# One core, a hybrid decoder layer: the keys' norms and scaling moved into the last projection of a head, the masks of the inverse issued one level ahead, the retention's decayed keys bound to program order

## Chip, core and metric

The kernel runs on one core of one Trainium2 chip. The metric is the device time of one execution in microseconds (us). Three runs of the kernel before gave 2976.19, 2977.47 and 2981.94 us, a median of 2977.47 us.

## What is computed

One step of a one-layer decoder on 2048 prompt rows, 16 learned meta rows in front of them, and 8 x 4 rows of sampling, 1024 wide. The residual stream goes through one combined input projection into two groups of four heads: retention, and gated DeltaNet. Then come an output projection, a layer norm, a SwiGLU feed-forward part of width 2816 and a last layer norm. The change lies in the DeltaNet group, with one line in the retention group. Cut to that:

```python
def l2_norm(x):
    return x * lax.rsqrt(jnp.sum(jnp.square(x), -1, keepdims=True) + RMS_EPS)
...
gk = l2_norm(conv[..., W:2 * W].reshape(bsz, L, H_GDN, HEAD_DIM))
beta = jax.nn.sigmoid(gb.astype(f32))
...
decay = jnp.exp(jnp.where(incl, G[..., :, None] - G[..., None, :], -jnp.inf))
kk = jnp.einsum('bnhid,bnhjd->bnhij', k, k)
lower = jnp.where(strict, kk * decay, 0.0) * beta[..., :, None]
a_mat = jnp.eye(C, dtype=q.dtype) + lower
...
sol = lax.linalg.triangular_solve(a_mat, rhs, left_side=True, lower=True, unit_diagonal=True)
...
k_d = k * jnp.exp(log_gamma[:, None] * (C - 1.0 - idx))[..., None]
```

The last line is of the retention group. A chunk is 128 rows.

## The kernel before

**Stages.** The attention part runs from the start to about 1310 us of the trace, the output projection and the feed-forward part fill the rest. The change touches the attention part only. It goes over four blocks (b0 to b3) of 512 prompt rows; b0 carries the 48 meta and sampling rows as well. In each block the projections of eight heads follow each other, in b0 to b2 as r0 g0 r1 g1 r2 g2 r3 g3 (r: retention, g: DeltaNet), in b3 as r0 g0 g1 r1 g2 g3 r2 r3.

**Projections fill PE.** A projection is a row of k-steps of three matmuls (L406), a product of high and low parts. A retention projection (`ret_proj`) takes tiles of 128 rows and eight k-steps of 256 columns each; a DeltaNet projection (`gdn_proj`) has four parts, q, k, v and the gate z, each of eight k-steps of 512 columns. After q, k and v come a convolution over four rows and a SiLU, on ACT and DVE (L860 to L871). `flip` (L804) transposes q or k on PE (L810), takes sums of squares on ACT (L813) and, for k, copies the transposed keys `kp` to SBUF on DVE (L817). It is called at step 5 of the k part for q, and at step 5 of the z part for k. Behind all four parts stand the norms: `rsqrt` (three Newton steps of small DVE instructions, L266 to L278) and the two scale vectors `gsk` (L875, L876).

**Chains lie among the projections.** When the projection of g is through, its chain (`gdn_chain`, `gdn_group`) starts. It is a generator that yields a nominal time from the list `LAT` after each piece; `advance` hands it the time of the k-steps that go by. So its pieces lie among the k-steps of the next projections, stretched by a factor from `pace`: 0.9 x 25 us x (heads until the next g) / `INVERSE`, for two heads 0.9 x 25 x 2 / 21 = 2.14. A chain begins with the decays (`mg` on DVE L918, L921 on PE, the exponential on ACT L925, two maskings on POOL L926 and L927), scales the keys (`kp`, DVE L935), transposes and scales v (PE L938, DVE L939), transposes the scaled keys (PE L943, ACT L945), forms kT x kT (PE L949) and the masked matrix `LT` (DVE L951). From it come `Z` and `U` on DVE (L960, L961), and on POOL, in one loop (L963), the six masked matrices `Lm` of the six levels. Each level then takes a product (L973), a correction on DVE (L975) and two products (L980, L982). Two refinements follow (L993 to L1003). In the second half of the chain the four chunks are scanned: L1035 and L1036 on PE, `r` on DVE (L1038), L1043 on PE, `u` on ACT, L1052 and L1054 on PE, the new state and `O` on DVE (L1053, L1055), `kt` on DVE (L1022). The second half of one head's chain runs beside the first half of the next one's.

**Other work on DVE and POOL there.** In b0 to b2 the layer norm of the next block's rows is issued during r1, g1, r2 and g2 at steps 18 and 26 (`LN_AT`), that is in the z part of g1 and of g2: statistics and multiplication on DVE (L289, L307), two additions on POOL (L309). A tile of a retention projection needs two rotary products on DVE (L571, L572) and an addition on POOL (L573). The retention chain (`ret_chain`) has in its `flip` the decayed keys `rkd` (DVE L634).

**What sets the order.** The code is traced in the order above, and then a scheduler lays each engine's instructions into a fixed row by its own estimate of when each can start: what was traced first goes first if it is ready, otherwise something later passes it. On the chip each engine takes its row strictly in order. `keep_in_program_order` binds an instruction behind the one that was traced last on its engine. PSUM tiles `w` have three buffers, the projections' `pj` two.

Of the kernel before, what the change touches and what calls it, by code (L numbers as in the profile page):

```python
# [8 lines left out]
F32 = mybir.dt.float32  # L9
# [4 lines left out]
ALU = mybir.AluOpType  # L14
# [4 lines left out]
HD = 128  # L19
# [220 lines left out]
class Builder:  # L240
# [372 lines left out]
    def ret_chain(self, b, h, qkvg, mixd):  # L613
# [12 lines left out]
        def flip(t):  # L626
            rows, c0, ch = tiles[t]
            pp = self.prt.tile([128, 4, 128], F32, tag="rt", name="rt")
            for a in range(2):
                nc.tensor.transpose(pp[:, a, :rows], qk[t][:, a, :], self.ident[:rows, :rows])  # L630
            qkT = mp.tile([128, 2, 128], F32, tag="rqkT", name="rqkT")[:, :, :rows]
            nc.scalar.copy(out=qkT, in_=pp[:, 0:2, :rows])
            kd = mp.tile([128, 128], F32, tag="rkd", name="rkd")[:rows]
            nc.vector.tensor_scalar(out=kd, in0=qk[t][:, 1, :], scalar1=col("kdm" if ch < 0 else "kd", rows), scalar2=None, op0=ALU.mult)  # L634
            st[t] = [pp, qkT[:, 0], qkT[:, 1], kd]
# [152 lines left out]
    def gdn_proj(self, b, h, G, out):  # L788
# [15 lines left out]
        def flip(a):  # L804

            for ts in sets:
# [7 lines left out]
                if a:  # L814
# [3 lines left out]
                    kps.append(kp)  # L818

        for piece in range(2):  # L820
            wh, wl = self.next_piece()
            for part in range(2):
# [9 lines left out]
                for (c0, n) in groups:  # L832
# [17 lines left out]
                if which < 3:  # L850
# [21 lines left out]
                    cv.append(o)  # L872
        rn = self.rsqrt(sq.rearrange("p a b -> p (a b)"), 2 * nt, 128, self.sm, 1.0, 4.0 * RMS_EPS).rearrange("p (a b) -> p a b", a=2)
        sk = self.sm.tile([128, 2, nt], F32, tag="gsk", name="gsk")
        nc.vector.tensor_scalar(out=sk[:, 0], in0=rn[:, 0], scalar1=HD ** -0.5, scalar2=None, op0=ALU.mult)  # L875
        nc.vector.tensor_tensor(out=sk[:, 1], in0=rn[:, 1], in1=G["sb"][:, :, h], op=ALU.mult)  # L876
        out += [cv, zg, sk, kps]

# [19 lines left out]
    def gdn_group(self, b, h, cv, zg, sk, kp, G, mixd, ts, tiles):  # L898
# [16 lines left out]


        mg = big("mg")[:R, :, :R]
        nc.vector.tensor_tensor(out=mg, in0=bc(M1), in1=G["g"][:R, ts[0]:ts[0] + m, h].unsqueeze(2).broadcast_to([R, m, R]), op=ALU.mult)  # L918
        pe = wide()
        for i in range(m):  # L920
            nc.tensor.matmul(pe[:R, i, :R], lhsT=U1, rhs=mg[:, i, :], start=True, stop=True)  # L921
        yield LAT[6]
        E = big("E", 2)[:R, :, :R]
# [3 lines left out]
        nc.gpsimd.tensor_tensor(out=E, in0=E, in1=bc(M1), op=ALU.mult)  # L927


        kp = kp[:R]  # L930
        vb = big("vb", 2, n=128)[:R]
        lane = lambda a: a.unsqueeze(2).broadcast_to([R, m, 128])
        here = slice(ts[0], ts[0] + m)
        cq = sk[:R, 0, here]
        nc.vector.tensor_tensor(out=kp, in0=kp, in1=lane(sk[:R, 1, here]), op=ALU.mult)  # L935
        p = wide()[:R, :m, :]
        for i in range(m):
            nc.tensor.transpose(p[:, i, :], v[:, col(i):col(i) + R], self.ident)  # L938
        nc.vector.tensor_tensor(out=vb, in0=p, in1=lane(G["sv"][:R, here, h]), op=ALU.mult)  # L939
        yield LAT[7]  # L940
        pk = wide()
        for i in range(m):
            nc.tensor.transpose(pk[:, i, :R], kp[:, i, :], idn)  # L943
        kT = big("kT", 2)[:, :, :R]
        nc.scalar.copy(out=kT, in_=pk[:, 0:m, :R])  # L945
        yield LAT[8]
        pl = wide()
# [13 lines left out]
        nc.vector.scalar_tensor_tensor(out=U, in0=L0, scalar=-1.0, in1=Ib, op0=ALU.mult, op1=ALU.add)  # L961
        for x in range(1, nl):
            nc.gpsimd.tensor_tensor(out=Lm[:, x - 1], in0=LT, in1=lvl(x), op=ALU.mult)  # L963
        yield LAT[9]
        pt = wide()[:R, :m, :R]
# [3 lines left out]
        for x in range(1, nl):  # L969
            yield LAT[10]  # L970
            py = wide()[:R, :m, :R]
            for i in range(m):
                nc.tensor.matmul(py[:, i, :], lhsT=Lm[:, x - 1, i, :], rhs=T[:, i, :], start=True, stop=True)  # L973
            Z = big("Z", 2, F16)[:R, :, :R]
            nc.vector.scalar_tensor_tensor(out=Z, in0=py, scalar=-1.0, in1=Ib, op0=ALU.mult, op1=ALU.add)  # L975
            yield LAT[11]
            pt = wide()[:R, :m, :R]
            pu = wide()[:R, :m, :R]
            for i in range(m):
                nc.tensor.matmul(pt[:, i, :], lhsT=U[:, i, :], rhs=Z[:, i, :], start=True, stop=True)  # L980
# [8 lines left out]
        nc.scalar.copy(out=V, in_=U)
        yield LAT[12]  # L990
        pe = wide()[:R, :m, :R]
# [5 lines left out]
        for it in range(2):  # L997
            yield LAT[13]
            pu = wide()[:R, :m, :R]
            for i in range(m):  # L1000
                nc.tensor.matmul(pu[:, i, :], lhsT=Er[:, i, :], rhs=V[:, i, :], start=True, stop=True)
            V = big(f"V{it}", 1, F32 if it else F32R)[:R, :, :R]
            nc.vector.tensor_tensor(out=V, in0=U, in1=pu, op=ALU.add)  # L1003
# [14 lines left out]
        for i in range(m):  # L1018
# [19 lines left out]
            nc.vector.scalar_tensor_tensor(out=r[:orow], in0=pp[:orow, 0, :], scalar=gc("ng", i, orow), in1=vb[:orow, i, :], op0=ALU.mult, op1=ALU.add)  # L1038
# [631 lines left out]
```

## Time and profile before

| what | value |
|---|---|
| median of three runs | 2977.47 us |
| the profiled execution | 2978.62 us |
| its span in the trace | 2976.8 us |
| mean granted clock of PE | 0.985 |

The profiled execution lies 0.04% above the median. Its span is 1.8 us shorter than its time. In the rows of the trace a time is counted from the start of the span; a DVE instruction's start can lie a few hundredths of a us before the end of the one ahead of it. A row of the timeline gives start, length, engine, line, operation, what it writes and reads, and in brackets the idle time ahead of it with what ended it.

### The profile page before, as it was taken

How to read it: one execution, taken by the hardware profiler on the slowest of the kernel's cores; microseconds unless marked ns; L12 is line 12 of the kernel's file. 1: busy time of each engine (PE TensorE's matmuls, PEld its weight loads, DVE VectorE, ACT ScalarE, POOL GpSimd, SP SyncE). 2: the span in 40 equal slices, each digit the busy share in tenths (PEclk: the TensorE clock that was granted, in tenths of full speed). 3: DMA queues.
4: the chain of work that ended last, by engine and by line, in shares of the span. 5: the costliest groups of instructions: out<-in, count | busy, mean ns of one | idle time of the engine just before them, and what ended most of it. 6: DMA issues, size and time to landing. Idle time of an engine off the chain costs nothing. (4 is left out here: it accounts for less than half of the span.)

```text
span 2976.8 us, 47482 instructions
## 1 busy us (share of the span) xinstructions
PE 2854.8 (96%) x17942; PEld 2550.5 (86%) x17942; DVE 1938.3 (65%) x4218; ACT 996.7 (33%) x2351; POOL 778.0 (26%) x757
## 2 busy tenths in 40 slices
PE   6999999999999999989989999999999999999997
PEld 6977888888888878877778999999999999989886
DVE  7777777776776676757776776667544444854447
ACT  2434344444444454432233333333211111321221
POOL 1312222221222112215544434433200101411111
PEclk8989999999999999999999999999999999999999
DMA  7544534444344333346768766667755555787762
GB/s 259 202 163 150 201 136 156 149 169 150 135 155 181 136 120 125 120 146 215 243 203 281 278 230 223 233 234 260 274 182 186 177 181 185 272 292 242 240 227 94
DMA packets 223093, 580.89 MB, mean 195 GB/s; under 512 B 27296, under 2 KB 62672, under 8 KB 206480
## 3 DMA queue, kind: packets, MB, share of 16 engines
q1 hardware_dynamic: 222864, 577.86, 55.8%
q8 instruction: 141, 2.31, 0.3%
q14 instruction: 88, 0.72, 0.1%
HBM read 409.48 MB, written 168.30 MB: 194 GB/s over the span
## 5 line engine op out<-in xcount | busy, mean ns | idle before, releaser
L406 PE MATMUL pj<-wh,xT 128*128 128x256 f32 (+2 forms) x2176 | 458.9, 295 | 7.4 <-ACT wh L349 3.0
L406 PE MATMUL pj<-xT,wh 128*128 128x512 f32 (+1 forms) x1280 | 379.7, 380 | 1.8 <-ACT cpre L846 1.0
L406 PEld LDWEIGHTS pj<-wh,xT 128*128 128x128 f32 (+1 forms) x2176 | 353.0, 188 | 12.4 <-ACT wh L349 3.3
L1507 DVE TENSOR_TENSOR y<-y,d 128x512 f32<-128x512 f32 (+1 forms) x344 | 234.9, 683 | 172.7 <-PE d L406 172.6
L406 PE MATMUL pj<-wl,xT 128*128 128x256 f32 (+3 forms) x1088 | 310.2, 285 | 0.9 <-POOL wl L356 0.5
L406 PE MATMUL d<-dh,fh 128*128 128x512 f32 (+1 forms) x745 | 295.9, 397 | 6.5 <-DVE y L1505 6.5
L406 PE MATMUL d<-dh,fl 128*128 128x512 f32 (+1 forms) x745 | 294.2, 395 | 0.0
L406 PE MATMUL d<-dl,fh 128*128 128x512 f32 (+1 forms) x745 | 292.2, 392 | 0.0
L356 POOL TENSOR_TENSOR fl<-ta,fh 128x384 fp32r<-128x384 f32 (+1 forms) x65 | 64.2, 987 | 738.7 <-issue 541.9
L406 PEld LDWEIGHTS pj<-xT,wh 128*128 128x128 f32 x1280 | 211.9, 194 | 25.3 <-issue 3.4
L406 PE MATMUL pj<-xT,wl 128*128 128x512 f32 (+1 forms) x640 | 229.8, 359 | 0.0
L406 PEld LDWEIGHTS pj<-wl,xT 128*128 128x128 f32 (+1 forms) x1088 | 204.5, 188 | 1.7 <-POOL wl L356 0.8
L406 PEld LDWEIGHTS d<-dh,fl 128*128 128x128 f32 (+1 forms) x745 | 136.6, 183 | 38.1
L406 PEld LDWEIGHTS d<-dh,fh 128*128 128x128 f32 (+1 forms) x745 | 136.7, 183 | 25.1 <-DVE y L1505 7.1
L406 PEld LDWEIGHTS d<-dl,fh 128*128 128x128 f32 (+1 forms) x745 | 136.7, 183 | 19.0
L406 PEld LDWEIGHTS pj<-xT,wl 128*128 128x128 f32 x640 | 122.7, 192 | 16.8 <-issue 0.8
L862 DVE SCALAR_TENSOR_TENSOR cacc<-cpre,cw,cacc 128x512 f32<-128x512 f32 (+1 forms) x144 | 115.7, 804 | 32.6 <-ACT cacc L860 31.1
L963 POOL TENSOR_TENSOR Lm<-LT,lvl 128x512 f16<-128x512 f32 (+1 forms) x108 | 129.3, 1231 | 11.3 <-DVE LT L951 10.5
L1405 DVE TENSOR_TENSOR u<-x,Y 128x384 f32<-128x384 f32 (+1 forms) x132 | 67.5, 511 | 97.0 <-PE Y L406 96.9
L349 ACT CAST fh<-ta 128x384 fp32r<-128x384 f32 (+1 forms) x66 | 31.8, 482 | 292.1 <-DVE ta L1413 292.1
L406 PE MATMUL W<-t,a22h 128*128 128x384 f32 (+1 forms) x528 | 124.4, 321 | 4.3 <-ACT t L349 4.3
L406 PE MATMUL Z<-b,s34h 128*128 128x384 f32 (+1 forms) x520 | 123.6, 323 | 4.6 <-ACT b L349 4.6
(392 smaller groups left out, 7168.8 us busy)
## 6 DMA issues: line engine op xcount, KB each, us to landing
wh<-parts SPq DMA_DIRECT2D x45, 1024.0 KB, 5.1
wl<-parts SPq DMA_DIRECT2D x45, 1024.0 KB, 6.8
fr<-dn SPq DMA_DIRECT2D x66, 512.0 KB, 5.3
fr<-gu SPq DMA_DIRECT2D x44, 512.0 KB, 4.6
s12h<-wd SPq DMA_DIRECT2D x44, 512.0 KB, 4.6
s12l<-wd SPq DMA_DIRECT2D x44, 512.0 KB, 5.6
s34h<-wd SPq DMA_DIRECT2D x44, 512.0 KB, 4.0
s34l<-wd SPq DMA_DIRECT2D x44, 512.0 KB, 4.9
```

What stands on the lines that cost most here:

```text
L349: i = nc.scalar.copy(out=h, in_=src)
L356: i = (nc.vector if el == "dve" else nc.gpsimd).tensor_tensor(out=l, in0=src, in1=h.bitcast(F32), op=ALU.subtract)
L406: self.nc.tensor.matmul(out, lhsT=a(k), rhs=b(k), start=first and k == 0 and i == 0, stop=last and k == kn - 1 and i == 2, skip_group_chec ...
L862: nc.vector.scalar_tensor_tensor(out=ac, in0=pre[:, i:i + N], scalar=w(i), in1=ac, op0=ALU.mult, op1=ALU.add)
L963: nc.gpsimd.tensor_tensor(out=Lm[:, x - 1], in0=LT, in1=lvl(x), op=ALU.mult)
L1405: add = lambda o, x, p: nc.vector.tensor_tensor(out=o, in0=x, in1=p, op=ALU.add)
L1507: nc.vector.tensor_tensor(out=ys, in0=ys, in1=p, op=ALU.add)
```

## The change

Seven edits stand in the diff. The norms become a function `norms` that is called inside the z part, at step 6 of its eight (b1 to b3) or step 4 of its last column group (b0), and that scales `kp` as well. The flip of k is called at step 0 of the z part (b0: step 2 of the first column group). The chain starts with the transposes of the keys and of v, then the decays, and the products kT x kT follow the decays' product without a yield between. The masks of level x + 1 are issued with the product of level x, only the first one with `LT`. `LAT` and `INVERSE` follow the new pieces: 19.4 in place of 21, so that `pace` gives 2.32 where it gave 2.14. The decayed keys `kd` are bound to program order. The number of instructions of each kind stays as it was.

```diff
-LAT = [1.0, 0.7, 0.7, 0.7, 2.0, 0.7, 0.5, 1.2, 1.8, 1.8, 1.0, 1.0, 1.7, 1.0, 0.6, 0.5, 0.5, 1.2]
+LAT = [1.0, 0.7, 0.7, 0.7, 2.0, 0.7, 0.9, 2.8, 1.0, 1.0, 1.7, 1.0, 0.6, 0.5, 0.5, 1.2]
...
-INVERSE = 21.0
+INVERSE = 19.4
...
-            nc.vector.tensor_scalar(out=kd, in0=qk[t][:, 1, :], scalar1=col("kdm" if ch < 0 else "kd", rows), scalar2=None, op0=ALU.mult)
+            i = nc.vector.tensor_scalar(out=kd, in0=qk[t][:, 1, :], scalar1=col("kdm" if ch < 0 else "kd", rows), scalar2=None, op0=ALU.mult)
+            self.tc.keep_in_program_order(i)
...
+        def norms():
+
+            rn = self.rsqrt(sq.rearrange("p a b -> p (a b)"), 2 * nt, 128, self.sm, 1.0, 4.0 * RMS_EPS).rearrange("p (a b) -> p a b", a=2)
+            sk = self.sm.tile([128, 2, nt], F32, tag="gsk", name="gsk")
+            nc.vector.tensor_tensor(out=sk[:, 1], in0=rn[:, 1], in1=G["sb"][:, :, h], op=ALU.mult)
+            for kp, ts in zip(kps, sets):
+                r = tiles[ts[0]][0]
+                here = slice(ts[0], ts[0] + len(ts))
+                nc.vector.tensor_tensor(out=kp[:r], in0=kp[:r], in1=sk[:r, 1, here].unsqueeze(2).broadcast_to([r, len(ts), 128]), op=ALU.mult)
+            nc.vector.tensor_scalar(out=sk[:, 0], in0=rn[:, 0], scalar1=HD ** -0.5, scalar2=None, op0=ALU.mult)
+            sks.append(sk)
...
-                        if i == 5 and which % 2 and c0 == groups[-1][0]:
-                            flip(which // 2)
+                        if which == 1 and i == 5 and c0 == groups[-1][0]:
+                            flip(0)
+                        if which == 3 and c0 == 0 and i == (2 if b == 0 else 0):
+                            flip(1)
+                        if which == 3 and c0 == groups[-1][0] and i == (4 if b == 0 else 6):
+                            norms()
...
+        pk = wide()
+        for i in range(m):
+            nc.tensor.transpose(pk[:, i, :R], kp[:, i, :], idn)
+        kT = big("kT", 2)[:, :, :R]
+        nc.scalar.copy(out=kT, in_=pk[:, 0:m, :R])
         mg = big("mg")[:R, :, :R]
...
+        yield LAT[6]
         pe = wide()
         for i in range(m):
             nc.tensor.matmul(pe[:R, i, :R], lhsT=U1, rhs=mg[:, i, :], start=True, stop=True)
-        yield LAT[6]
...
-        nc.vector.tensor_tensor(out=kp, in0=kp, in1=lane(sk[:R, 1, here]), op=ALU.mult)
...
-        for x in range(1, nl):
-            nc.gpsimd.tensor_tensor(out=Lm[:, x - 1], in0=LT, in1=lvl(x), op=ALU.mult)
-        yield LAT[9]
+        masked = lambda x: nc.gpsimd.tensor_tensor(out=Lm[:, x - 1], in0=LT, in1=lvl(x), op=ALU.mult)
+        masked(1)
+        yield LAT[7]
...
+            if x + 1 < nl:
+                masked(x + 1)
             Z = big("Z", 2, F16)[:R, :, :R]
```

How the rows of the engines move is shown at the chain of head g1 in block b1 (at 571 us in the trace), which starts among the tiles of r2's projection. Rows of L406 are k-steps; line numbers of the changed kernel are some 10 higher than those of the one before.

On PE before, where the chain comes to the transposes of the keys (L943); the decays' product L921 and the transposes of v, L938, stand eight and seven rows ahead of this piece:

```order
L1052 MATMUL sc<-u,kt 128x128
L1054 MATMUL w<-u,E 128x128
L406 MATMUL pj<-wh,xT 128x256
L406 MATMUL pj<-wl,xT 128x256
L406 MATMUL pj<-wh,xT 128x256 x2
L943 MATMUL w<-ident,kp 128x128 x4
```

On PE after, the same place; L934 are the transposes of the keys, L946 those of v, L951 the decays' product, L959 kT x kT:

```order
L406 MATMUL pj<-wh,xT 128x256 x2
L406 MATMUL pj<-wl,xT 128x256
L934 MATMUL w<-ident,kp 128x128 x4
L946 MATMUL w<-ident,post 128x128 x4
L951 MATMUL w<-mg,cb 128x128 x4
L959 MATMUL w<-kT 128x128 x4
L406 MATMUL pj<-wh,xT 128x256 x2
L406 MATMUL pj<-wl,xT 128x256
```

The keys' transposes now come first, and the four groups of the chain's start stand side by side with no k-step between them.

On DVE before, the end of the row of work that leads to the scaled keys (L935); the layer norm's multiplication L307 stands eight rows ahead of this piece:

```order
L572 TENSOR_TENSOR rotB<-pj,rott 128x256
L278 SCALAR_TENSOR_TENSOR rqy<-rqt,rqy 128x8
L939 TENSOR_TENSOR vb<-w,sv 128x512
L875 TENSOR_SCALAR gsk<-rqy 128x4
L876 TENSOR_TENSOR gsk<-rqy,sb 128x4
L634 TENSOR_SCALAR rkd<-qk,cb 128x128
L935 TENSOR_TENSOR kp<-kp,gsk 128x512
```

On DVE after, from the layer norm's multiplication on; L829 scales the keys, L947 scales v, L961 makes `LT`, L970 makes `Z`:

```order
L307 TENSOR_TENSOR xa<-xa 128x1024
L825 TENSOR_TENSOR gsk<-rqy,sb 128x4
L830 TENSOR_SCALAR gsk<-rqy 128x4
L572 TENSOR_TENSOR rotB<-pj,rott 128x256
L829 TENSOR_TENSOR kp<-kp,gsk 128x512
L1065 SCALAR_TENSOR_TENSOR S_gdn_298<-S_gdn_298,eg,sc 128x128
L1067 SCALAR_TENSOR_TENSOR O<-qs,eg,w 128x128
L1034 TENSOR_SCALAR kt<-kp,eg 128x128
L947 TENSOR_TENSOR vb<-w,sv 128x512
L961 TENSOR_TENSOR LT<-w,mg 128x512
L571 TENSOR_TENSOR qk<-pj,rott 128x256
L970 TENSOR_TENSOR Z<-LT,lvl 128x512
```

Gone from ahead of the scaled keys are `vb` and `rkd`; the layer norm stands right ahead of them still. Behind this piece follow L572, L971 (`U`) and then L1050 (`r` of the scan).

On ACT before, around the sums of squares of k (L813); L864 is the tanh of v's convolution:

```order
L987 COPY Uf<-w 128x512
L989 CAST mg<-Uf 128x512
L864 ACTIVATE cth<-cacc 128x512
L813 ACTIVATE junk,gsq<-pj 128x128 x4
L848 ACTIVATE zg<-pj 128x512
```

On ACT after, where L814 are the sums of squares and L882 is that tanh:

```order
L999 COPY Uf<-w 128x512
L1001 CAST mg<-Uf 128x512
L814 ACTIVATE junk,gsq<-pj 128x128 x2
L882 ACTIVATE cth<-cacc 128x512
L814 ACTIVATE junk,gsq<-pj 128x128 x2
L866 ACTIVATE zg<-pj 128x512
```

Two of the four sums now stand ahead of the tanh. On POOL the maskings of this chain stand as L955, L956, four masks L972, one rotary addition, two masks; before they stood as L926, L573, L927, two L573, six masks L963.

More of the change, by code (lines that the diff above doesn't have):

```diff
@@ L818, in flip @@
                     kps.append(kp)
+        def norms():
[8 more added lines that the diff above has]
+            sks.append(sk)
+        sks = []
         for piece in range(2):
@@ L872, in gdn_proj @@
                     cv.append(o)
[L873 to L877, printed above, removed]
+        out += [cv, zg, sks[0], kps]
     def gdn_chain(self, b, h, cvz, G, mixd):
@@ L914, in gdn_group @@
         Ib, Ih, idn = bc(self.ident[:R, :R]), self.identh[:R, :R], self.ident[:R, :R]
+        kp = kp[:R]
+        pk = wide()
[3 more added lines that the diff above has]
+        nc.scalar.copy(out=kT, in_=pk[:, 0:m, :R])
         mg = big("mg")[:R, :, :R]
         nc.vector.tensor_tensor(out=mg, in0=bc(M1), in1=G["g"][:R, ts[0]:ts[0] + m, h].unsqueeze(2).broadcast_to([R, m, R]), op=ALU.mult)
+        vb = big("vb", 2, n=128)[:R]
+        lane = lambda a: a.unsqueeze(2).broadcast_to([R, m, 128])
+        here = slice(ts[0], ts[0] + m)
+        cq = sk[:R, 0, here]
+        p = wide()[:R, :m, :]
+        for i in range(m):
+            nc.tensor.transpose(p[:, i, :], v[:, col(i):col(i) + R], self.ident)
+        nc.vector.tensor_tensor(out=vb, in0=p, in1=lane(G["sv"][:R, here, h]), op=ALU.mult)
+        yield LAT[6]
         pe = wide()
@@ L927, in gdn_group @@
         nc.gpsimd.tensor_tensor(out=E, in0=E, in1=bc(M1), op=ALU.mult)
[L930 to L946, printed above, removed]
         pl = wide()
@@ L969, in gdn_group @@
         for x in range(1, nl):
-            yield LAT[10]
+            yield LAT[8]
             py = wide()[:R, :m, :R]
@@ L973, in gdn_group @@
                 nc.tensor.matmul(py[:, i, :], lhsT=Lm[:, x - 1, i, :], rhs=T[:, i, :], start=True, stop=True)
+            if x + 1 < nl:
+                masked(x + 1)
             Z = big("Z", 2, F16)[:R, :, :R]
             nc.vector.scalar_tensor_tensor(out=Z, in0=py, scalar=-1.0, in1=Ib, op0=ALU.mult, op1=ALU.add)
-            yield LAT[11]
+            yield LAT[9]
             pt = wide()[:R, :m, :R]
@@ L989, in gdn_group @@
         nc.scalar.copy(out=V, in_=U)
-        yield LAT[12]
+        yield LAT[10]
         pe = wide()[:R, :m, :R]
@@ L997, in gdn_group @@
         for it in range(2):
-            yield LAT[13]
+            yield LAT[11]
             pu = wide()[:R, :m, :R]
@@ L1036, in gdn_group @@
                 nc.tensor.matmul(po[:, 1, :], lhsT=q[:, c0:c0 + R], rhs=S, start=True, stop=True)
-            yield LAT[14]
+            yield LAT[12]
             nc.vector.scalar_tensor_tensor(out=r[:orow], in0=pp[:orow, 0, :], scalar=gc("ng", i, orow), in1=vb[:orow, i, :], op0=ALU.mult, op1=ALU.add)
@@ L1044, in gdn_group @@
             nc.scalar.copy(out=u, in_=pp[:R, 2, :])
-            yield LAT[15]
+            yield LAT[13]
             if sp:
@@ L1059, in gdn_group @@
             nc.scalar.activation(out=junk, in_=O[:orow, i, :], func=AF.Square, scale=cq[:orow, i:i + 1], accum_out=ss[:orow, i:i + 1])
-            yield LAT[16]
+            yield LAT[14]
         rs = self.rsqrt(ss[:orow], m, orow, self.sm, 1.0 / HD, RMS_EPS)
@@ L1064, in gdn_group @@
         nc.vector.tensor_tensor(out=O[:orow], in0=O[:orow], in1=rs.unsqueeze(2).broadcast_to([orow, m, 128]), op=ALU.mult)
-        yield LAT[17]
+        yield LAT[15]
         for i in range(m):
```

## The prediction

> **What bounds the kernel now.** I read the page first, then PE's waits and the engines by stage, then the timelines at one head.
>
> ```profile
> PE 2854.8 (96%) x17942; PEld 2550.5 (86%) x17942; DVE 1938.3 (65%) x4218; ACT 996.7 (33%) x2351; POOL 778.0 (26%) x757
> 100.00:1310.00 1210.00, 1159.47 (x8656) 1020.39 (x8655) 847.73 (x2344) 525.17 (x1532) 285.70 (x362) 0.98 0.41 150
> PE w L943 <- DVE kp L935: 13.8, 7, 2.6
> PE w L980 <- DVE Z L975: 4.6, 4, 1.2
> PE w L967 <- DVE U L961: 1.3, 2, 0.6
> ```
>
> PE is the bound: 96% busy, and the change alters none of its instructions, only their order. It can win no more than PE's idle time. In the attention part behind the first 100 us that is 1210 - 1159.5 = 50.5 us. The row that the change aims at is the third: the transposes of the keys waited seven times, 13.8 us, for the scaling of the keys on DVE. Four of the seven are alike; they belong to g1 and g2 in b1 and b2. A stretch of 30 us around each:
>
> ```profile
> 555.00:585.00 30.00, 26.88 (x194) 24.99 (x192) 24.16 (x62) 8.46 (x24) 10.07 (x10) 0.94 0.30 110
> 628.00:658.00 30.00, 26.87 (x209) 24.99 (x209) 25.48 (x65) 9.36 (x28) 11.26 (x11) 1.00 0.43 147
> ```
>
> PE idles 3.12 and 3.13 us here. In the first stretch the granted clock is 0.94, so 0.06 x 30 = 1.8 us more are lost; in the second, with the same idle time, nothing. Two of the four such stretches had that loss.
>
> **Why the keys are late.** PE, DVE and POOL in the first stretch:
>
> ```profile
> 561.41 0.40 PE L406 MATMUL pj<-wh,xT 128*128 128x256 f32 x2
> 561.76 0.40 PE L406 MATMUL pj<-wh,xT 128*128 128x256 f32 x2
> 567.64 1.16 PE L921 MATMUL w<-mg,cb 128*128 128x128 f32 x8 [0.22 <-DVE V L1003]
> 568.95 0.66 PE L938 MATMUL w<-ident,post 128*128 128x128 f32 x4
> 569.44 0.39 PE L1043 MATMUL sc<-r,V 128*128 128x128 f32 x2
> 574.00 0.79 PE L943 MATMUL w<-ident,kp 128*128 128x128 f32 x4 [2.55 <-DVE kp L935]
> 558.52 1.28 DVE L289 BATCH_NORM_STATS2 lnst<-xa 128x6 f32<-128x512 f32 x2
> 564.30 0.17 DVE L278 SCALAR_TENSOR_TENSOR rqy<-rqt,rqy 128x8 f32<-128x8 f32 x1
> 565.69 1.23 DVE L307 TENSOR_TENSOR xa<-xa 128x1024 f32<-128x1024 f32 x1
> 567.50 0.79 DVE L278 SCALAR_TENSOR_TENSOR rqy<-rqt,rqy 128x8 f32<-128x8 f32 x1
> 568.82 0.70 DVE L276 TENSOR_TENSOR rqt<-rqy 128x8 f32<-128x8 f32 x1
> 569.78 1.03 DVE L277 SCALAR_TENSOR_TENSOR rqt<-rqt,rqa 128x8 f32<-128x8 f32 x1
> 571.14 0.68 DVE L939 TENSOR_TENSOR vb<-w,sv 128x512 f32<-128x512 f32 x1
> 571.74 0.23 DVE L875 TENSOR_SCALAR gsk<-rqy 128x4 f32<-128x4 f32 x1
> 571.99 1.27 DVE L634 TENSOR_SCALAR rkd<-qk,cb 128x128 f32<-128x128 f32 x1
> 573.18 0.68 DVE L935 TENSOR_TENSOR kp<-kp,gsk 128x512 f32<-128x512 f32 x1
> 566.99 2.50 POOL L309 TENSOR_TENSOR xa<-xa 128x512 f32<-128x512 f32 x2 [9.45 <-DVE rqt L277]
> 569.51 1.28 POOL L926 TENSOR_TENSOR mg<-E,cb 128x512 f32<-128x512 f32 x1
> 571.91 1.26 POOL L927 TENSOR_TENSOR E<-E,cb 128x512 f32<-128x512 f32 x1
> ```
>
> The first two rows are a k-step apart, 0.35. DVE has no gap from 558.52 to 573.86. Three of the norms' instructions that take 0.17 elsewhere (the row at 564.30) take 0.79, 0.70 and 1.03, and each ends where a POOL instruction ends: 568.29, 569.52 and 570.81, against two of 1.25 from 566.99 and the one to 570.79. `rkd` ends at 573.26, POOL's L927 at 573.17. So DVE lost 0.62 + 0.54 + 0.86 = 2.0 us in the norms and, with 1.19 up to the next start where 0.2 would do, 1.0 in `rkd`: 3.0 together, about what PE idles. The instructions between that read PSUM, `vb` for one, kept their 0.68.
>
> The Trainium skill, page "SBUF — State Buffer", section "Who interferes with whom", says why: a DVE instruction with two SBUF inputs and a GpSimd instruction that reads SBUF exclude each other, and the one issued first holds the ports to its end. The trace agrees, with the four ends above. By this rule alone the new place of the norms is not safe: the layer norm's additions come where they did.
>
> **The keys' scaling within the projection.** In the order on DVE the scaling (L829) keeps its place behind the layer norm. Gone from ahead of it are `vb` (571.74 - 571.14 = 0.60), `rkd` (1.19) and, since the decays now come later, the blocked time of the norms (2.0): 3.8 us. Two things come instead. Two sums of squares now stand on ACT ahead of v's tanh:
>
> ```profile
> 556.31 0.62 ACT L989 CAST mg<-Uf 128x512 fp32r<-128x512 f32 x1
> 557.24 0.64 ACT L864 ACTIVATE cth<-cacc 128x512 f32<-128x512 f32 x1 [0.31 <-DVE cacc L862]
> 558.54 0.28 ACT L813 ACTIVATE junk<-pj 128x128 f32<-128x128 f32 x1 [0.67 <-PE pj L810]
> 558.94 0.28 ACT L813 ACTIVATE junk<-pj 128x128 f32<-128x128 f32 x1
> ```
>
> A sum takes 558.94 - 558.54 = 0.40. Two behind 556.93 end at 557.7, the tanh at 558.4, the other two at 559.2; only then can the copy of `kp` (0.6) run, which now stands ahead of the statistics. These start at 559.8, 1.3 later, less the 0.6 of the copy that no longer comes behind: 0.7 late. Second, the scaling has two SBUF inputs and stands four rows behind L307, so it waits for the first addition on POOL: that starts when L307 ends and takes 1.25, of which two `gsk` and one rotary product cover 0.4: 0.85. The keys are scaled at 573.86 - 3.8 + 0.7 + 0.85 = 571.6.
>
> PE comes earlier too. It lacks L921 (1.16) and L938 (569.44 - 568.95 = 0.49), has four matmuls of k-steps more (0.47), and waited before for 3.12 - 2.55 = 0.6 on the way: 574.00 - 2.55 - 0.6 - 1.2 = 569.7. It idles 1.9 where it idled 3.1. **The wait moves to L934 and shrinks by 1.2 us a head, it doesn't go.** Bounds: without either delay 0.3; if the second addition also passes the keys, 3.1. I take 1.9. For b0, whose three waits make 13.8 - 4 x 2.55 = 3.6 us, the same share: 1.4. Together -4 x 1.2 - 1.4 = **-6.2 us** (-13.8 to 0).
>
> **The chain's new start.** L951 and L959 now follow the transposes at once, and `LT` (L961) needs the masked decays, which pass ACT and POOL in between. Rows for it, from g0 of b1 before:
>
> ```profile
> 507.10 1.05 PE L949 MATMUL w<-kT 128*128 128x128 f32 x8
> 513.11 0.38 PE L1043 MATMUL sc<-r,V 128*128 128x128 f32 x2
> 508.18 0.69 DVE L951 TENSOR_TENSOR LT<-w,mg 128x512 f32<-128x512 f32 x1
> 509.78 1.40 DVE L961 SCALAR_TENSOR_TENSOR U<-Z,ident 128x512 f16<-128x512 f16 x1
> 511.36 0.93 DVE L1022 TENSOR_SCALAR kt<-kp,eg 128x128 f32<-128x128 f32 x1
> 512.20 0.34 DVE L1038 SCALAR_TENSOR_TENSOR r<-sc,ng,vb 128x128 f32<-128x128 f32 x1
> 508.95 7.74 POOL L963 TENSOR_TENSOR Lm<-LT,lvl 128x512 f16<-128x512 f32 x6
> 568.83 0.60 ACT L925 ACTIVATE E<-w 128x512 f32<-128x512 f32 x1 [1.58 <-PE w L921]
> ```
>
> Here `r` ended 0.57 ahead of its matmul, although `U` (0.69 unblocked) and `kt` (0.27) had lost 1.4 to the masks. After, counted from the start of L934 in g1: 0.45 for it, 0.49 for v, 1.16 for L951, 0.6 for ACT, 1.3 for POOL make 4.1; `LT` to 4.8, the rotary product to 5.1; `Z` waits for POOL's second masking (to 5.4) and ends at 6.0; a rotary product; `U` waits for the first mask (to 7.0) and ends at 7.6; `r` at 7.9. PE is at that matmul after 0.45 + 0.49 + 1.16 + 1.05, 8.3 k-steps of 0.35 and 0.4 for the scan's two: 6.4. It waits 1.5 us. In g0's order the same count gives 1.0. DVE stands still while `LT` waits; queued behind it are the rotary products (which free `pj`), the state and `r`. Nothing in the trace of before shows this place, so the bounds are 0 and 1.5 in each of 16 chains, 0 to 24. I count the six whose order I have laid out, 4 x 1.5 + 2 x 1.0 = 8, less some 2 us of small waits behind it that fall away when PE is late: **+6 us**.
>
> **Masks and levels.** POOL takes the masks in a burst still (four, one rotary addition, two), since nothing but `LT` holds them: 0. The levels stand 2 x 2.32 = 4.64 us apart, not 2 x 2.14 = 4.29. Of the last two rows of the first fence, 5.9 us, I take half, **-3 us** (-5.9 to 0). `rkd` in program order costs what it did, 0.2 in place of 1.2 where POOL is not in its way; DVE is not waited for there: 0.
>
> **The clock.** Two of four heads lost 1.8. With 1.9 and 1.5 us idle within 10 us I expect no change (-3.6 to +3.6).
>
> The Trainium skill, page "TensorE: Matmul & The Clock Gate", part 1, says that the activity window runs free, about 3.4 us, whatever the kernel does. Equal idle time with and without a loss, as in the two stretches above, agrees.
>
> **Sum.** 2978.62 - 6.2 + 6 - 3 = 2975.4, say 2976 us. The profiled execution lies 1.2 us above the median of 2977.5, so against that it is -0.05%: no change that a measurement of this kernel can tell, which takes about 0.2%, or 6 us.
>
> **Rivals.**
> 1. The wait goes altogether: neither delay comes in, and `r` keeps its 0.57 us. Then -13.8, and the 3.6 of the clock: 2961. For it: the norms are traced earlier, and DVE is 70% busy in this part (847.7 of 1210), so most heads have room. Against it: DVE's row without a gap. Half of it, with the levels' 3, gives 2967, which also counts as faster.
> 2. Slower, by one mechanism: DVE stuck at L961 until POOL has masked the decays. If it costs 1.5 in the four heads and 1.0 in the other twelve, +18, with the -6.2 of the keys: 2990. It decides where `r` ends more than six k-steps, 2.1 us, behind its L1047. For it: `Z`, `U` and `kt` are blocked in turn, and before there was 0.57 to spare. Against it: I laid out two orders of sixteen, and a PE that waits gives DVE time for all that follows.
> 3. The masks don't do what the edit says, as counted above. Were they spread, `U` and `kt` would lose less; at 0.7 for `U` in 16 chains that is at most 11 us on DVE, on PE a part of rival 2. The order speaks against it; it is within the forecast.
>
> **Chances.** Forecast, within 6 us: 0.38. Rival 1, whole or half: 0.37. Rival 2: 0.25. The range leaves out a tenth on each side: 2962 to 2992, from nearly the whole of rival 1 to the whole of rival 2. The likeliest case alone has 2971 to 2983. Faster by over 0.2% 0.37, within 0.38, slower 0.25.
>
> **What would show it.** Keys: among PE's waits, L934 for `kp` at 1 to 2.5 us in the four heads; rival 1 has none. Squares: the tanh L882 starts at the end of two sums, not of the convolution. The start: PE waits at L1055 for `r` at over 0.5 us, and DVE has a gap ahead of L961 that ends with POOL; if DVE has no such gap, the +6 is wrong. Levels: the waits of L992 for `Z` under half of 4.6 us. What would break the prediction outright is a new wait outside these places, above all in b0 and b3, whose orders I have not laid out.

## The result and the profile after

The changed kernel takes 3010.01 us (median; 3007.91 to 3013.58), the kernel before 2976.83 us beside it: ratio 1.0111, 95% interval 1.0099 to 1.0123. It is slower by 1.1%, and outside the range of the prediction. The profiled execution took 3010.14 us, its span is 3008.4 us, 31.6 more than before; the mean granted clock is 0.979 in place of 0.985.

From the profile of after, PE's row of busy times, the row of the attention part by windows, and six of PE's waits (us in all, times, longest):

```profile
PE 2861.9 (95%) x17942; PEld 2559.3 (85%) x17942; DVE 1924.8 (64%) x4218; ACT 997.3 (33%) x2351; POOL 778.5 (26%) x757
100.00:1310.00 1210.00, 1138.32 (x8488) 1004.34 (x8489) 821.30 (x2305) 515.60 (x1505) 285.09 (x361) 0.98 0.40 147
PE sc L1055 <- DVE r L1050: 14.5, 12, 2.9
PE pj L406 <- DVE LT L961: 6.6, 1, 6.6
PE pt L525 <- DVE rotB L572: 3.8, 1, 3.8
PE rt L671 <- DVE rkd L634: 3.0, 4, 0.9
PE w L934 <- DVE kp L829: 2.9, 5, 0.7
PE w L992 <- DVE Z L987: 1.0, 2, 0.8
```

PE has the same 17942 instructions. It idles 3008.4 - 2861.9 = 146.5 us where it idled 122.0, and is busy 7.1 us longer. The keys' wait has shrunk from 13.8 to 2.9 us and the levels' from 4.6 to 1.0, as the edits meant. But new waits for DVE stand in the list, that for `r` above all: 14.5 us where it was 1.5. The groups of DVE's instructions that write `LT` and the first `Z`, with the duration as minimum, median and maximum in ns, and below them what ended DVE's idle time ahead of `LT`:

```profile
L961 DVE TENSOR_TENSOR LT<-w,mg x20: 188/692/694, 119.3 to 1263.3; 128x512 f32<-128x512 f32 x16, 48x48 f32<-48x48 f32 x4
L970 DVE TENSOR_TENSOR Z<-LT,lvl x20: 695/1141/7892, 121.6 to 1264.0; 128x512 f16<-128x512 f32 x16, 48x48 f16<-48x48 f32 x4
  POOL mg L955: 37.6, 17
```

DVE stands still 17 times, 37.6 us in all, for POOL's masking of the decays; with two small waits the view has 40.2 us. In the kernel before the same view has 2.3 us, all for PE. `Z` took 692 at the median before and takes 1141, once 7892.

**One ordinary head** (g1 of b2), from the timelines of DVE, POOL, ACT and PE:

```profile
883.47 0.69 DVE L947 TENSOR_TENSOR vb<-w,sv 128x512 f32<-128x512 f32 x1
886.36 0.69 DVE L961 TENSOR_TENSOR LT<-w,mg 128x512 f32<-128x512 f32 x1 [2.19 <-POOL mg L955]
887.30 0.95 DVE L970 TENSOR_TENSOR Z<-LT,lvl 128x512 f16<-128x512 f32 x1
888.17 0.41 DVE L572 TENSOR_TENSOR rotB<-pj,rott 128x256 f32<-128x256 f32 x1
888.50 1.30 DVE L971 SCALAR_TENSOR_TENSOR U<-Z,ident 128x512 f16<-128x512 f16 x1
889.73 0.34 DVE L1050 SCALAR_TENSOR_TENSOR r<-sc,ng,vb 128x128 f32<-128x128 f32 x1
885.04 1.28 POOL L955 TENSOR_TENSOR mg<-E,cb 128x512 f32<-128x512 f32 x1 [0.99 <-ACT E L954]
884.36 0.60 ACT L954 ACTIVATE E<-w 128x512 f32<-128x512 f32 x1 [0.35 <-PE w L951]
890.12 0.49 PE L1055 MATMUL sc<-r,V 128*128 128x128 f32 x2 [1.53 <-DVE r L1050]
```

`LT` stands right behind `vb` in DVE's row, while the decays have only just left PE: ACT takes them at 884.36, POOL to 886.3. DVE waits 2.19 us, then `Z` and `U` come, and only then `r` of the running scan. PE waits 1.53 us for it.

**Where along the kernel.** The last `r` of each block, read off DVE's rows of that line, gives each block's length (us in the profiled executions); "old start" is a kernel of the experiments (e4), the change with the chain's start of before. The start of the next block's first chain lies ahead of that `r`, and is counted with the block it lies in:

| | b0 | b1 | b2 | b3 | the rest |
|---|---|---|---|---|---|
| before | 518.3 | 287.0 | 287.4 | 192.2 | 1691.9 |
| after | 537.1 | 292.5 | 291.4 | 194.3 | 1693.1 |
| old start | 517.0 | 281.2 | 281.5 | 189.9 | 1692.6 |

Over half of the loss, 18.8 us, lies in b0. Its largest piece is one gap:

```profile
119.86 1.80 DVE L356 TENSOR_TENSOR wl<-raw,wh 128x1024 fp32r<-128x1024 f32 x1
121.59 7.89 DVE L970 TENSOR_TENSOR Z<-LT,lvl 128x512 f16<-128x512 f32 x1
130.13 0.41 DVE L571 TENSOR_TENSOR qk<-pj,rott 128x256 f32<-128x256 f32 x1
120.55 1.70 POOL L573 TENSOR_TENSOR qk<-qk,rotB 48x256 f32<-48x256 f32 x1
122.22 6.72 POOL L972 TENSOR_TENSOR Lm<-LT,lvl 128x512 f16<-128x512 f32 x6
131.02 0.55 PE L406 MATMUL pj<-wh,xT 128*128 128x256 f32 x1 [6.63 <-DVE LT L961]
```

A split of weights came between `LT` and `Z`. So `Z` met POOL's rotary addition and then all six masks, which follow each other without a gap to 128.94, and ended at 129.48. The rotary products behind it free `pj`, and PE waited 6.63 us for that. (The view names `LT` as releaser; the products at 130.13 and just behind are what freed the buffer.) Before, `Z` stood right behind `LT` in this head and took 0.69.

### The profile page after: what moved, and what is told of

It reads as the page before. It is cut to its first block, busy times and chain, and to the rows that moved or that the text cites. A ratio compares the mean times of both kernels' runs of the same rounds, so it can differ in the third digit from the quotient of the medians.

```text
span 3008.4 us, 47469 instructions
## 1 busy us (share of the span) xinstructions
PE 2861.9 (95%) x17942; PEld 2559.3 (85%) x17942; DVE 1924.8 (64%) x4218; ACT 997.3 (33%) x2351; POOL 778.5 (26%) x757
## 5 line engine op out<-in xcount | busy, mean ns | idle before, releaser
L406 PE MATMUL pj<-wh,xT 128*128 128x256 f32 (+2 forms) x2176 | 458.3, 296 | 14.3 <-DVE LT L961 6.6
L406 PE MATMUL pj<-xT,wh 128*128 128x512 f32 (+1 forms) x1280 | 380.2, 381 | 3.2 <-DVE kp L818 1.3
L406 PEld LDWEIGHTS pj<-wh,xT 128*128 128x128 f32 (+1 forms) x2176 | 355.1, 190 | 17.3 <-issue 6.8
L406 PE MATMUL pj<-wl,xT 128*128 128x256 f32 (+3 forms) x1088 | 311.9, 287 | 0.5 <-POOL wl L356 0.5
L406 PE MATMUL d<-dh,fh 128*128 128x512 f32 (+1 forms) x745 | 296.6, 398 | 7.9 <-DVE y L1517 7.9
L406 PE MATMUL d<-dh,fl 128*128 128x512 f32 (+1 forms) x745 | 294.8, 396 | 0.0
L406 PE MATMUL d<-dl,fh 128*128 128x512 f32 (+1 forms) x745 | 292.9, 393 | 0.0
L406 PEld LDWEIGHTS pj<-xT,wh 128*128 128x128 f32 x1280 | 211.2, 194 | 28.4 <-ACT junk L814 4.5
L406 PE MATMUL pj<-xT,wl 128*128 128x512 f32 (+1 forms) x640 | 230.6, 360 | 0.0
L406 PEld LDWEIGHTS pj<-wl,xT 128*128 128x128 f32 (+1 forms) x1088 | 206.8, 190 | 1.2 <-POOL wl L356 0.8
L406 PEld LDWEIGHTS d<-dh,fl 128*128 128x128 f32 (+1 forms) x745 | 137.1, 184 | 38.2
L406 PEld LDWEIGHTS d<-dh,fh 128*128 128x128 f32 (+1 forms) x745 | 137.0, 184 | 26.6 <-DVE y L1517 8.4
L406 PEld LDWEIGHTS d<-dl,fh 128*128 128x128 f32 (+1 forms) x745 | 137.1, 184 | 19.2
L406 PEld LDWEIGHTS pj<-xT,wl 128*128 128x128 f32 x640 | 123.0, 192 | 17.2 <-issue 0.8
L972 POOL TENSOR_TENSOR Lm<-LT,lvl 128x512 f16<-128x512 f32 (+1 forms) x108 | 128.9, 1223 | 0.2 <-DVE LT L961 0.2
L406 PE MATMUL W<-t,a22h 128*128 128x384 f32 (+1 forms) x528 | 124.4, 321 | 4.1 <-ACT t L349 4.1
L406 PE MATMUL Z<-b,s34h 128*128 128x384 f32 (+1 forms) x520 | 123.0, 322 | 3.9 <-ACT b L349 3.9
```

Source lines behind the costliest of these rows:

```text
L406: self.nc.tensor.matmul(out, lhsT=a(k), rhs=b(k), start=first and k == 0 and i == 0, stop=last and k == kn - 1 and i == 2, skip_group_chec ...
L972: masked = lambda x: nc.gpsimd.tensor_tensor(out=Lm[:, x - 1], in0=LT, in1=lvl(x), op=ALU.mult)
```

## The experiments

The theories. **Head**: the chain's new start stops DVE at `LT`, and what is queued behind it makes PE late. **Pin**: the bound `rkd`. **Norms**: the earlier norms and transposes disturb the projection. **Masks**: the masks one level ahead come late. The first four kernels undo or do one part each.

| kernel | us | ratio to before, 95% interval | DVE idle ahead of LT, us | PE waits for r, us |
|---|---|---|---|---|
| before | 2976.83 | | 2.3 | 1.5 |
| after | 3010.01 | 1.0111 (1.0099 to 1.0123) | 40.2 | 14.5 |
| e1, after without the pin | 3025.48 | 1.0156 (1.0141 to 1.0171) | 26.3 | 15.1 |
| e2, before with the pin | 2981.55 | 1.0010 (1.0001 to 1.0020) | 2.8 | 1.5 |
| e3, after, masks at once | 3011.88 | 1.0112 (1.0095 to 1.0128) | 43.3 | 14.5 |
| e4, after, old start | 2964.03 | 0.9947 (0.9932 to 0.9962) | 2.1 | none |
| e5, after, one yield more | 2976.26 | 0.9986 (0.9977 to 0.9996) | 15.7 | 2.6 |
| e6, e4 with the new pace | 2962.87 | 0.9939 (0.9923 to 0.9954) | 20.5 | 1.9 |
| e7, after, decays first | 2986.23 | 1.0018 (1.0009 to 1.0027) | 6.3 | 8.3 |
| e8, e4 without the pin | 2962.47 | 0.9939 (0.9924 to 0.9954) | 0.6 | 0.7 |
| e9, before with the norms alone | 2962.94 | 0.9940 (0.9926 to 0.9954) | 0.7 | 0.7 |
| e10, after, old start in b0 | 2989.54 | 1.0034 (1.0021 to 1.0048) | 26.8 | 8.1 |
| e11, after, one masking on DVE | 2991.56 | 1.0037 (1.0027 to 1.0048) | none | 6.6 |
| e12, after, masks in two buffers | 3009.73 | 1.0094 (1.0077 to 1.0112) | 31.3 | 14.5 |

The last two columns are from the view of `LT`'s group and from PE's waits, each in one profiled execution; the medians of the kernel before in the four sessions were 2976.83 to 2980.77 us. So a difference between two rows of the table can be off by some 4 us. The text gives differences in us; by the ratios, the 46, 34, 24 and 18 us that it names for the start (e4, e5, e7, e11) come to 49, 37, 28 and 22.

### e1 and e2: the pin alone

```diff
             i = nc.vector.tensor_scalar(out=kd, in0=qk[t][:, 1, :], scalar1=col("kdm" if ch < 0 else "kd", rows), scalar2=None, op0=ALU.mult)
-            self.tc.keep_in_program_order(i)
```

> The changed kernel with the retention's decayed keys left free to move; all else as changed. Head theory (the chain's new start puts DVE behind POOL and costs most of the 33 us): the pin is worth its own waits at L671, 3 to 4 us in four places, so 3004 to 3011 us. Pin theory (the bound keys delay the retention's chain and that lets TensorE idle and lose clock): 20 us or more come back, at most 2990 us. Norms theory (keys' transposes and norms earlier in the projection disturb it): 3005 to 3011. Mask theory: 3005 to 3011.

> The kernel before with the retention's decayed keys bound to program order, and nothing else. Head, norms and mask theories: 2975 to 2983 us (at most the 3 to 4 us of waits at L671). Pin theory: 2995 us or more.

All four theories missed e1: without the pin the changed kernel is 15.5 us slower still. PE's waits, DVE and POOL of e1 (g1 of b1) show why:

```profile
PE sc L1046 <- DVE S_gdn L1064: 16.0, 12, 2.1
594.52 0.34 DVE L1049 SCALAR_TENSOR_TENSOR r<-sc,ng,vb 128x128 f32<-128x128 f32 x1
598.59 1.16 DVE L634 TENSOR_SCALAR rkd<-qk,cb 128x128 f32<-128x128 f32 x1 [3.73 <-POOL qk L573]
600.33 0.33 DVE L1064 SCALAR_TENSOR_TENSOR S_gdn<-S_gdn,eg,sc 128x128 f32<-128x128 f32 x1
592.43 5.42 POOL L971 TENSOR_TENSOR Lm<-LT,lvl 128x512 f16<-128x512 f32 x4
597.81 0.74 POOL L573 TENSOR_TENSOR qk<-qk,rotB 128x256 f32<-128x256 f32 x1
```

Left free, `rkd` is laid ahead of the scan's state. It needs a rotary addition that stands behind four masks on POOL, so DVE waits 3.73 us, and PE waits for the state 12 times. The pin puts `rkd` behind. It is no cause of the loss; it keeps the new start from costing more. In the order of before there is nothing for it to save: e2 is 0.1% slower than before, with an interval that starts at 0.01%, and e8 below is e4 without the pin within the intervals.

### e3: the masks at once

```diff
-        masked(1)
+        for x in range(1, nl):
+            masked(x)
...
-            if x + 1 < nl:
-                masked(x + 1)
```

> The changed kernel with all six masks issued at once behind the first level, as before; all else as changed. They stood as one burst on POOL in most heads of both traces, so head, pin and norms theories: 3005 to 3015 us. Mask theory (spreading them makes each level wait for POOL): 2990 us or less.

3011.88 us; the intervals of e3 and of after cover each other. The mask theory falls as worded: on POOL the masks run as a burst wherever the code issues them, since nothing but `LT` holds them.

### e4: the old start with the rest of the change

The decays, then the values, then the keys' transposes, with the four yields and the pacing of before; `kp` stays scaled in the projection.

```diff
+        mg = big("mg")[:R, :, :R]
...
+        pe = wide()
...
+        yield LAT[6]
+        E = big("E", 2)[:R, :, :R]
...
         nc.vector.tensor_tensor(out=vb, in0=p, in1=lane(G["sv"][:R, here, h]), op=ALU.mult)
+        yield LAT[7]
+        pk = wide()
...
+        yield LAT[8]
         pl = wide()
```

> The changed kernel with the chain's start of before (decays first, then values, then keys' transposes, with the yields and the pacing of before), but the keys still scaled inside the last projection, the masks one level ahead and the decayed keys bound. Head theory: the 25 to 30 us go, 2970 to 2985 us. Pin, norms or mask theory: 3000 us or more.

2964.03 us: the norms theory falls, the new start costs 46 us, and what is left of the change is faster than before by 0.5%. No theory had named a time that low: not only the loss goes. DVE and POOL in g1 of b2:

```profile
853.78 0.34 DVE L1053 SCALAR_TENSOR_TENSOR r<-sc,ng,vb 128x128 f32<-128x128 f32 x1
857.48 0.69 DVE L964 TENSOR_TENSOR LT<-w,mg 128x512 f32<-128x512 f32 x1
858.20 0.69 DVE L973 TENSOR_TENSOR Z<-LT,lvl 128x512 f16<-128x512 f32 x1
849.85 1.28 POOL L940 TENSOR_TENSOR mg<-E,cb 128x512 f32<-128x512 f32 x1
```

The masked decays are there 6.4 us ahead of `LT`, and `r` has gone before it. By the table of blocks the start cost 20.1 us in b0, 11.3 and 9.9 in b1 and b2, 4.4 in b3. Of the 46.2 us between the spans, 37.1 are PE's idle time (146.5 against 2962.2 - 2852.8 = 109.4) and 9.1 PE's busy time at the same instructions.

### e5, e6 and e7: what about the start costs

e5 keeps the changed order and adds a yield between the decays and the keys' product (of `LAT`, here and for e6, the changed numbers alone are shown):

```diff
-0.9, 2.8, 1.0, 1.0, 1.7
+0.9, 1.4, 1.4, 1.0, 1.0, 1.7
...
         nc.gpsimd.tensor_tensor(out=E, in0=E, in1=bc(M1), op=ALU.mult)
+        yield LAT[7]
         pl = wide()
```

> The changed kernel with one more place to interleave: a yield between the masked decays and the keys' product, its 1.4 us taken from the 2.8 us behind it, so that the pacing's sum stays. The start's order is as changed. Cover theory (LT is set right behind the decays, so DVE stops at LT until ACT and POOL have passed the decays on, and all of DVE's queue with it): with projection work between, most of the 46 us between the changed kernel and the one with the old start come back, 2965 to 2985 us. Order theory (the decays come too late in the chain, behind keys and values, wherever the yields are): 2995 to 3012. Pacing theory (the smaller sum of the pacing numbers moves the chain's steps against the projection): 3005 to 3012.

e6 is e4 with the pacing's sum of the changed kernel:

```diff
-0.5, 1.2, 1.8, 1.8,
+0.5, 0.8, 1.2, 1.2,
...
-INVERSE = 21.0
+INVERSE = 19.4
```

> The kernel with the old start (which took 2964 us), but paced to the changed kernel's sum: the start's four numbers 0.5, 0.8, 1.2 and 1.2 in place of 0.5, 1.2, 1.8 and 1.8, and 19.4 in place of 21.0 for the whole inverse. Cover and order theories: 2960 to 2970 us. Pacing theory: 2995 us or more.

e7 moves the decays to the front of the changed start, and adds no yield:

```diff
+        mg = big("mg")[:R, :, :R]
+        pe = wide()
...
+        nc.gpsimd.tensor_tensor(out=Es, in0=E, in1=bc(ST), op=ALU.mult)
+        nc.gpsimd.tensor_tensor(out=E, in0=E, in1=bc(M1), op=ALU.mult)
         kp = kp[:R]
         pk = wide()
```

> The changed kernel with the decays (their matmuls, the exponential and both maskings) moved ahead of the keys' and the values' transposes; the yields and the pacing are as changed. Order theory: LT finds the decays done, so most of the 46 us come back, 2965 to 2985 us. Cover theory: the yield of 0.9 us and the transposes now stand between the decays and LT, so DVE waits less: 2975 to 2995 us. Pacing theory: 3005 to 3012 us.

Pacing falls: e6 is e4 within the intervals. The yield alone brings 34 of the 46 us back, with the decays as late in the code as in the changed kernel. Decays first bring 24, a part, as the cover theory had it; DVE hardly stands still ahead of `LT` then (6.3 us), but in g1 and g2 of b1 and b2 `r` still stands behind `LT`, `Z` and `U`, and PE waits 8.3 us for it in all.

e6 says what a stop of DVE costs. DVE's row, and PE's wait for `r`:

```profile
569.07 0.34 DVE L1053 SCALAR_TENSOR_TENSOR r<-sc,ng,vb 128x128 f32<-128x128 f32 x1
571.21 0.69 DVE L964 TENSOR_TENSOR LT<-w,mg 128x512 f32<-128x512 f32 x1 [1.79 <-POOL qk L573]
PE sc L1058 <- DVE r L1053: 1.9, 3, 1.2
```

DVE idles 20.5 us ahead of `LT` in e6, half as much as in the changed kernel, and the time is as low as any here, within the 4 us that the intervals leave. **A stop of DVE need not cost anything; what is queued behind it does.** Here `r` is ahead. By itself e6 leaves a rival: 13.3 of its 20.5 us are waits for PE, which works on meanwhile, and DVE waits for PE elsewhere in e4 (2.46 us ahead of a rotary product in the head shown above). e7 speaks against it: its 6.3 us are all waits for PE, `r` stands behind, and it takes 22 us more than e4.

### e8 and e9: what is left of the change

e8 is e4 with the line of the pin taken out. e9 is the kernel before with one part of the change, the function `norms` as in the diff above, its call and the two flips in their new places, and without

```diff
-        nc.vector.tensor_tensor(out=kp, in0=kp, in1=lane(sk[:R, 1, here]), op=ALU.mult)
```

in the chain.

> The kernel with the old start, and the retention's decayed keys left free as before. The pin was worth 15 us in the changed kernel and nothing that can be told in the kernel before. If it is worth something only where DVE stops in the chain's start: 2960 to 2968 us. If it always saves the decayed keys from the back of DVE's queue once the keys are scaled in the projection: 2972 to 2985 us.

> The kernel before with one part of the change alone: keys' transposes and the norms earlier in the last projection, the keys scaled there. Chain's start, masks and decayed keys as before. If this part brings the whole gain of the kernels with the old start: 2959 to 2968 us. If the masks one level ahead bring a part of it: 2968 to 2975 us.

e4, e6, e8 and e9 are alike within their intervals: the norms' part brings the whole gain by itself, 0.6% (0.46 to 0.74%), and masks and pacing add nothing that can be told. e9 beats both kernels. PE's row, and two of its three largest waits for DVE in the attention part of e9 (the third, for the scan's `O`, is 4.8 us where it was 4.3):

```profile
PE 2850.6 (96%) x17942; PEld 2546.2 (86%) x17942; DVE 1929.1 (65%) x4218; ACT 991.9 (33%) x2351; POOL 785.1 (27%) x757
PE pt L525 <- DVE zg L866: 5.2, 3, 2.3
PE w L993 <- DVE Z L988: 4.6, 4, 1.2
```

No row for the keys is left: in the old order the transposes of the keys come last in the start, and by then the keys are scaled. PE idles 110.9 us, 11.1 less than before, though a new wait of 5.2 us takes a part of the 13.8 back; and it is busy 4.2 us less.

### e10, e11 and e12: three pieces of the price

e10 has the old start and its pacing in b0 alone (`if b == 0:` around the two starts).

> The changed kernel with the old start and its pacing in the first block alone. By the last r of each block the first block lost 20.1 us to the old start's kernel and the later ones 26. If these are prices of the places themselves: 2985 to 2995 us. If the first block's loss comes from elsewhere (its projection's rows, the bound keys), or the later blocks take it over: 3000 us or more.

2989.54 us. Its b0 takes 517.4 us, that of e4; its b1, b2 and b3 take 292.6, 291.3 and 194.3, those of after. The price is paid in each place by itself.

e11 takes POOL out of the way to `LT`:

```diff
-        nc.gpsimd.tensor_tensor(out=Es, in0=E, in1=bc(ST), op=ALU.mult)
+        nc.vector.tensor_tensor(out=Es, in0=E, in1=bc(ST), op=ALU.mult)
```

> The changed kernel with the first masking of the decays (the one that LT needs) on DVE in place of POOL. If POOL's part of the way to LT is what holds DVE up: DVE's wait before LT falls from 40 us to about half, and the time to 2990 to 3002 us. If any stop of DVE in the chain's start costs the same, whichever engine it waits for: 3004 to 3015 us.

2991.56 us: 18 of the 46 us come back, as the first theory had it. The view of the group `mg` has what DVE waits for now, a quarter of the 40 us where half was expected; PE's wait for `r` is less than half:

```profile
  ACT E L954: 10.4, 12
PE sc L1055 <- DVE r L1050: 6.6, 12, 0.9
```

With a shorter stop and the same order behind it the loss is smaller, so where `r` stands behind, the length of the stop counts too. The 5.9 us gap of PE in the first head is still there: `Z` is held for 7.91 us, though DVE has not stood still ahead of `LT`.

e12 has two buffers for the masks, so that POOL cannot run ahead of the levels:

```diff
-        Lm = mp.tile([128, nl - 1, m, R], F16, tag=pre + "Lm", name="Lm", bufs=1)[:R]
+        Lm = {}
...
+        def masked(x):
+            Lm[x] = mp.tile([128, m, R], F16, tag=pre + "Lm", name="Lm", bufs=2)[:R]
+            nc.gpsimd.tensor_tensor(out=Lm[x], in0=LT, in1=lvl(x), op=ALU.mult)
```

> The changed kernel with two buffers for the masked levels in place of one for all six, so that POOL can't run them off in one go but follows the levels. If the burst of masks on POOL is what held DVE's first level for 7.89 us in the first head, and the gap of 6.6 us behind it: that gap goes, 2998 to 3006 us. If POOL's masks then come late for the levels: 3008 to 3025 us.

3009.73 us, what the changed kernel takes; each theory has half. DVE and POOL in the first head, and two of PE's waits:

```profile
125.76 3.45 DVE L970 TENSOR_TENSOR Z<-LT,lvl 128x512 f16<-128x512 f32 x1
126.39 2.28 POOL L975 TENSOR_TENSOR Lm<-LT,lvl 128x512 f16<-128x512 f32 x2
PE pj L406 <- DVE LT L961: 2.2, 1, 2.2
PE sc L1083 <- DVE O L1080: 11.7, 7, 2.5
```

With two masks in the burst `Z` takes 3.45 and the gap is 2.2 us: the burst was its cause, and b0 is 9.8 us shorter (527.3). But b1, b2 and b3 are longer by 2.6, 3.8 and 1.2 us, and PE waits longer for the scan's `O` (7.2 us in the changed kernel). Why, is not shown; that the masks come late for the levels there would fit.

## Why the prediction was wrong

**The step that failed is the size of the chain's new start: +6 us, where the runs show 46.** The mechanism was named, as rival 2, with a chance of a quarter and a price of 2990 us. In the four heads g1 and g2 of b1 and b2 its count was right to a tenth: PE waits 1.53 to 1.54 us at L1055 where 1.5 was forecast (the five terms up to POOL's masking make 4.0, not 4.1, and `LT` starts 3.98 us after L934). In the two heads g0 it waits 0.53 and 0.52 where 1.0 was forecast. Three things went wrong in the size.

- The bounds took PE's wait for `r` as the whole price of DVE's stop, "0 and 1.5 in each of 16 chains". In all, the waits for `r` stay inside them, 14.5 us in 12 waits, though two of b0 take 2.85 and 2.74. But they are 14.5 of the 37.1 us that PE idles more than in e4. Another 10.4 are two gaps of b0, 6.63 us for `pj` and 3.80 behind `rotB`, each behind a `Z` that POOL's masks held (7.89 us, and 3.22 us for that of the 48 rows at 439.37). The rest is spread over many waits. The prediction wrote "queued behind it are the rotary products (which free `pj`), the state and `r`", and then priced `r` alone, and it let POOL hold a DVE instruction for one of its own at most. So each of those four heads, priced at 1.5, lost 2.7 us against e4 by its last `r`, and 2.1 to 2.2 against e6.
- It counted six chains of sixteen, "whose order I have laid out". The ten others were not free, and here lies most of the loss. Against e4, b0 lost 20.1 us, b3 4.4, and the chains of g3, which run into the next block, about 5 each in b1 and b2.
- "A PE that waits gives DVE time for all that follows" did not hold. By e6 DVE's waits are free where `r` stands ahead; in the changed order no such slack came.

Not all of the new waits belong to the start. The scan's `O` waits as long in e6, which has the old start and the new pacing, and loses nothing by it:

```profile
PE sc L1079 <- DVE O L1076: 7.2, 7, 1.5
PE sc L1082 <- DVE O L1079: 7.3, 7, 1.5
```

The first row is of the changed kernel, the second of e6.

**The keys: -6.2 forecast, -10.9 in the row.** The wait moved to L934 and shrank from 13.8 to 2.9 us; in the four heads it is 0.64 to 0.66, between the 1.9 of the forecast and the 0.3 that it gave for neither delay. One of the two delays held, the other did not. DVE and ACT of after, g1 of b1:

```profile
588.21 1.52 DVE L829 TENSOR_TENSOR kp<-kp,gsk 128x512 f32<-128x512 f32 x1
574.00 2.33 DVE L880 SCALAR_TENSOR_TENSOR cacc<-cpre,cw,cacc 128x512 f32<-128x512 f32 x3 [2.23 <-ACT cacc L878]
576.08 0.28 ACT L814 ACTIVATE junk<-pj 128x128 f32<-128x128 f32 x1
576.36 0.64 ACT L882 ACTIVATE cth<-cacc 128x512 f32<-128x512 f32 x1
```

The scaling takes 1.52, 0.84 more than its 0.68 of before: POOL's addition is in its way, as counted (0.85). Two sums of squares stand ahead of the tanh, as said, but the convolution ends at 576.33, when they do: the 0.7 did not come. And the part is worth more than its row. Alone (e9) it shortens the span by 15.3 us, of which 4.2 are PE's busy time at the same instructions; the prediction had put the clock at nothing. The 15.3 are near what rival 1 gave, 13.8 for the keys and 3.6 for the clock. In the kernel before, a stretch at half clock lies right behind the keys' wait of the first head, which ends at 574.00 (the granted clock is the third figure from the end):

```profile
571.00:585.00 14.00, 11.45 (x86) 11.28 (x86) 9.04 (x22) 1.61 (x6) 6.10 (x6) 0.88 0.17 56
585.50:588.90 3.40, 3.40 (x33) 3.39 (x32) 1.07 (x4) 1.17 (x4) 3.40 (x5) 1.00 0.82 279
```

From 574.3 to 577.7 the granted clock is 0.50, on both sides of it 1.00; e9 has 1.00 from 500 to 690. That the wait brings the slow clock is likely, not shown: two of the four such heads had none.

**Masks: 0, held** (e3). **Levels: -3.** The wait for `Z` fell below half, as forecast, 4.6 to 1.0, but no time that can be told came of it: e6, with the new pace, and e4, without, are alike. Their intervals are some 4 us wide to each side, so 3 us can't be told either way.

**The pin: 0, wrong in its reason.** "DVE is not waited for there" is true of before only: in the changed kernel PE waits 3.0 us for `rkd`. And there the pin is worth 15.5 us (e1).

**The clock: 0.** PE is busy 7.1 us longer with the same instructions, at a mean clock of 0.979 in place of 0.985. That is twice the bound of 3.6. Against e4 it is 9.1 us, so a part of the start's price is slower matmuls; which waits brought that about is not shown.

**Rival 3** (the masks do not spread) was right and harmless by e3. Its price of spreading, "a part of rival 2", was too simple: spread by force (e12), b0 gained 9.8 us and the later blocks gave 7.6 back.

The Trainium skill, page "SBUF — State Buffer", section "Who interferes with whom", gives the loser of the shared ports a wait for the whole instruction of the other engine. The ordinary head is in keeping: `U` takes 1.30 where 0.69 is its time alone, so it lost 0.61, less than the 1.36 of one mask there. The 7.89 us of the first head go beyond one instruction; there the loser waited for seven in a row.

## What to carry to other kernels

In all the rows shown DVE takes its instructions in the order laid out, so everything behind a waiting one waits too. So when an edit puts a consumer close behind a chain through two other engines, list what stands behind that consumer, price each of them, and in every stage, not only where the order has been laid out. Better, leave a place between the two for other work: one yield was worth 34 us here. And when an edit has several parts, run each alone: 0.6% lay in one of them, hidden under a loss more than twice as large.

## What the runs showed that was not expected

- A DVE instruction with two SBUF inputs was held for 7.89 us in place of 0.69, through a rotary addition and six masks on POOL; 7.91 again in e11, and 3.45 through the addition and two masks in e12. A `Z` of 48 rows took 3.22 us in the changed kernel's b0 and 0.19 in e5. The six masks took 6.72 us, 1.12 each, against 5.42 for four, 1.36 each, in e1 where DVE came in between. Why DVE got no turn between two masks here, and did elsewhere, stays open.
- 20.5 us of idle time on DVE ahead of one instruction cost nothing (e6), and 40.2 us at the same instruction were the mark of a loss of 46 (after). What stands behind the wait decides first; its length counts where `r` stands behind it (e11).
- A bound order that was neutral in one version (e8 against e4) was worth 15.5 us in another (e1 against after): `rkd` needs a rotary addition that stands behind the masks on POOL there. That the scheduler's estimate of its start missed this would fit; no run shows the estimate.
